# Making the delta-rule scan's operands beside the attention and loading them chunk by chunk

## The chip, the cores and the metric

The kernel runs on one core of a Trainium2 chip. It is written in Python against an explicit tile framework: the program allocates tiles in named pools, issues instructions to five engines (PE for matmuls, with a separate count PEld for its weight loads; DVE and ACT for element-wise work and reductions; POOL and SP, which here mostly issue DMA transfers), and a scheduler puts them into one fixed order per engine. The metric is the device time of one execution in microseconds; less is better.

## The reference, cut to what matters

One layer of a bidirectional trunk on 1024 tokens of width 1024, all in float32: a half-step feed-forward network, a mixing layer, a second half-step feed-forward network. The mixing layer projects its normed input once (`z = h @ w_in`). One part of the columns goes into attention (8 heads, three dilated bands), the other into RWKV-7, a delta-rule recurrence that runs forwards and backwards over the sequence, with its own decays and rates in each direction:

```python
u = u + mu_prev * (prev - u) + mu_next * (nxt - u)        # the "shift"
r, k, v, wd, ad, gd = jnp.split(u, cuts, axis=-1)         # receptance, key, value, low ranks
decay = jnp.exp(-jnp.exp(-jax.nn.softplus(-w_logit) - 0.5))
a = jax.nn.sigmoid(a0 + jnp.einsum('bsdr,drc->bsdc', ad, a2))
kk = kk / jnp.maximum(jnp.sqrt(jnp.sum(kk * kk, axis=-1, keepdims=True)), 1e-12)
k_dir = k[:, :, None, :] * (1.0 + (a - 1.0) * k_a)
...
def _rwkv7_step(state, inp):
    r, w, k, v, kk, kka = inp
    sa = jnp.einsum('dbhvk,dbhk->dbhv', state, kk)
    state = state * w[..., None, :] - sa[..., :, None] * kka[..., None, :] + v[..., :, None] * k[..., None, :]
    y = jnp.einsum('dbhvk,dbhk->dbhv', state, r)
```

`kk` is the normed key, `kka = kk * a` the rate, `k_dir` the key. The outputs of both directions are added, normed by group, given a bonus from `r`, `k_dir` and `v`, gated, and projected together with the attention's output.

## The kernel before, in words

**The scan in chunks.** The recurrence is not run token by token. The 1024 tokens are cut into 16 chunks of 64 (`C = 64`), two chunks to a block (`BLK = 2`, `TB = 128` tokens), 8 blocks, each in both directions. Channels lie on partitions: 512 channels are 4 tiles of 128, each a pair of heads of 64. With `cum` the running log decay inside a chunk, the chunk form needs four decayed operands: receptances `r * exp(cum)` and normed keys `kk * exp(cum one step earlier)` (the program's `pr`, side by side), rates and keys divided by the decay, `(1 + a) * kk * 0.5 * exp(-cum)` and `k_dir * exp(-cum)` (the program's `bk`), and the decay of the whole chunk, `gc`. From them come the matrix of products within a chunk (`lp`, masked to `lm`), whose inverse is built by doubling, and then the state goes from chunk to chunk.

**The order of the stages.** After the first feed-forward network and the low-rank projections, which store `cum` and the rates to DRAM (`lr_d`), comes the attention, 8 heads in a row (`attention`, with scores L713, bias and maximum L715, copies of the transposed weights L728, the last reduction `ss_a` of each head L763). After each head but the last `beside(h)` issues one stream of the RWKV projection (`project_rwkv` with `shift` and `stream`, L505 to L645), in the order `[4, 1, 5, 2, 6, 3, 7]`: column tiles 0 to 3 are receptances (0 comes earlier), 4 to 7 keys, 8 to 11 values. Then the scan begins: `prep` and `solve` of block 0, of block 1, the four value streams 8 to 11, and a loop over the blocks n with `merge`, `chain` and, ahead of need, `prep` and `solve` of block n + 3, with the projection of attended tokens among them (L1274 to L1333). The scheduler is free to weave these. The second feed-forward network follows.

**A key stream before.** ct 4 to 7 takes a shifted key tile of 128 channels x 1024 tokens (`us`). It loads the rates of both directions (`ra`, twice) and the receptances (`rr`) of the same channels. It makes the normed key `kr` (L611) and stores it. POOL adds the rates of the two directions (`rs`) and multiplies receptance by key (`rr`, L616); DVE multiplies the two (L618) for the bonus, which is stored. Then for each direction and each half of 512 tokens ACT makes `1 + (a - 1) * k_a` (L625) and DVE multiplies it by the key (`rb`, L626), stored by POOL; and for each direction DVE makes `(1 + a) * kr` over all 1024 tokens (`ra`, L628), stored by POOL.

**`prep` of a block before** (L818 to L876). For each direction SP loads `cum` (tile `th_w`), the rates `ka`, the keys `kd` (256 KB each) and receptances with normed keys (`in`, 512 KB). ACT makes `exp(cum)` (`e`, L840) and, in place, `exp(-cum)` (L841); DVE copies the chunks' last decay into `gc` (L843), and makes `pr` with two products (L845, L846; in the backward direction with a reversed view) and `bk` with two (L849, L851). A `bk` chunk has 192 columns: ACT copies the upper 64 partitions' rates behind the keys (L850), so that the odd head of a pair sees (keys, rates) where the even one sees (rates, keys). PE makes `lp` from `bk` and `pr` (L858), DVE masks (`lm`, L860), PE transposes `bk` (L866) and ACT copies that out (`bt`, L868). The PSUM pool of `prep` has three buffers. `solve` (L878 and on) runs its doubling on DVE (L894, L896); `merge` and `chain` hold the PE groups called st, y and xu; the state update on DVE is `sv` (L990).

**The value streams** (ct 8 to 11): shift (L537, L538), a reversed copy (L634), PE transposes (L640), ACT copies, and 8 stores each by SP.

The few lines of `prep` that the change takes out of the scan:

```python
A.activation(e4[:, :, :, 1:C + 1], chunks(cum), AF.Exp)
A.activation(flat(cum), flat(cum), AF.Exp, scale=-1.0)
ei = chunks(cum)
V.tensor_copy(gc[:, d], e4[:, :, :, C])
V.tensor_tensor(pt[:, :, :, 0:C], chunks(x["kk"]), e4[:, :, :, 0:C], op=OP.mult)
V.tensor_tensor(pt[:, :, :, C:], chunks(x["r"]), e4[:, :, :, 1:C + 1], op=OP.mult)
V.scalar_tensor_tensor(bb, chunks(ak[0]), 0.5, ei, op0=OP.mult, op1=OP.mult)
A.copy(bk[64:, :, :, 2 * C:], bk[64:, :, :, 0:C])
V.tensor_tensor(bk[:, :, :, C:2 * C], chunks(ak[1]), ei, op=OP.mult)
```

Of the kernel before, what the change touches and what calls it, by code (L numbers as in the profile page):

```python
# [10 lines left out]
F32 = mybir.dt.float32  # L11
F32R = mybir.dt.float32r
AF = mybir.ActivationFunctionType
# [150 lines left out]
class _Kernel:  # L164
# [340 lines left out]
    def project_rwkv(self, p, psum, x, blocks, wide=None):  # L505

        nc, V, A, T = self.nc, self.nc.vector, self.nc.scalar, self.nc.tensor
        for c0, n in blocks:
# [6 lines left out]
            if 4 <= c0 < 8:  # L515
                self.rates.append(wide.tile([128, S], F32, name="rs", tag="rr"))
            for ct in range(c0, c0 + n):
# [61 lines left out]
    def stream(self, p, psum, ct, y):  # L579
# [10 lines left out]
        elif ct < 8:  # L590
# [21 lines left out]
            self.nc.gpsimd.dma_start(self.rk_d[4 + i], kr)  # L612
            rates, r, both = self.rates[:2], *self.rates[2:]
            self.rates.clear()
            G.tensor_tensor(both, rates[0], rates[1][:, ::-1], op=OP.add)
            G.tensor_tensor(r, r, y, op=OP.mult)  # L616
# [3 lines left out]
            for d, a in enumerate(rates):  # L620
                turned = lambda z: z[:, ::-1] if d else z
                for half in range(2):
                    sl = slice(half * 512, half * 512 + 512)
                    b = p.tile([128, 512], F32, name="rb", tag="vts")
                    A.activation(b, a[:, sl], AF.Identity, scale=self.kah[:, i:i + 1], bias=self.ka1[:, i:i + 1])  # L625
                    V.tensor_tensor(b, b, turned(y)[:, sl], op=OP.mult)  # L626
                    self.nc.gpsimd.dma_start(self.ak_d[d][4 + i][:, sl], b)
                V.scalar_tensor_tensor(a, a, 1.0, turned(kr), op0=OP.add, op1=OP.mult)  # L628
                self.nc.gpsimd.dma_start(self.ak_d[d][i], a)
# [16 lines left out]


# [170 lines left out]
    def prep(self, n, p, psum, big):  # L818

        nc, V, A, T = self.nc, self.nc.vector, self.nc.scalar, self.nc.tensor  # L820
        flat = lambda z: z.rearrange("p a t -> p (a t)")
        chunks = lambda z: z.rearrange("p a (i t) -> p a i t", i=BLK)
        ls = slice(n * TB, (n + 1) * TB)
        lm = big.tile([128, 2, 2, BLK, 4, 128], F32, name="lm", tag="lm")
        gc = big.tile([128, 2, 4, BLK], F32, name="gc", tag="gc")
        blk = dict(lm=lm, pr=[], bt=[], gc=gc)
        for d in range(2):
            b = n if d == 0 else NC_ // BLK - 1 - n
            ts = slice(b * TB, (b + 1) * TB)
            cum = p.tile([128, 4, TB], F32, name="th_w", tag="th_w", bufs=2)  # L830
            self.load(cum, self.lr_d["w"][d][:, :, ls].rearrange("a p t -> p a t"))
            ak = [p.tile([128, 4, TB], F32, name=nm, tag=nm, bufs=b) for nm, b in (("ka", 2), ("kd", 1))]
            for j in range(2):
                self.load(ak[j], self.ak_d[d][4 * j:4 * j + 4, :, ls].rearrange("a p t -> p a t"))
# [640 lines left out]
```

## Time and profile before

Three runs took 2301.5, 2297.94 and 2296.86 us, median 2297.94. One execution was profiled; it gives no time of its own beside its span.

| | |
|---|---|
| median of the runs | 2297.94 us |
| span of the profiled execution | 2299.0 us |
| instructions in it | 41391 |
| PE busy (matmuls) | 2198.8 us, 96% |
| PE's weight loads | 1781.8 us, 77% |
| DVE busy | 1767.3 us, 77% |
| ACT busy | 1023.6 us, 45% |
| POOL busy | 537.0 us, 23% |

The stages lie in the span as follows: up to 915 us the first feed-forward network and the projections, 915 to 1183 the attention with the receptance and key streams, 1183 to 1292 the scan's start with the value streams, 1292 to 1480 its steady part, up to 1600 its last block and what follows it, and from 1700 the second feed-forward network.

In the lines of the profile a group is an engine, a line of the kernel, an operation, and the tile it writes with the tile it reads (out<-in); then partitions x elements, how many there were, busy time in us, mean ns of one. A wait is "engine, what it wanted to do and at which line <- the engine and line that it waited for". SP, POOL and the like with a "q" are queues of DMA transfers. Issuing a DMA is not counted in an engine's busy share, though a group of issues has a duration.

### The profile page before, as it was taken

The page shows a single profiled execution, that of the slowest core. Times are in us where ns is not written, and L with a number is a line of the kernel's source. Part 1 is how long each engine was busy: PE and PEld are TensorE (multiplying, and loading weights), DVE is VectorE, ACT ScalarE, POOL GpSimd, SP SyncE. Part 2 cuts the span into 40 slices and gives each one's busy share as a digit, 9 for nine tenths or more (in the row PEclk, how much of TensorE's full clock was granted, in tenths as well). Part 3 has the DMA queues.
Part 4 walks back from the last instruction along what each step waited for, and adds up shares of the span by engine and source line. Part 5 has one row for each costly group of instructions (what it writes and reads, how often), then busy time and mean ns, then how long its engine had stood idle before and what let it go on. Part 6 is the DMA issues. An engine that isn't in the chain of part 4 may idle for free. (4 is left out here: it accounts for less than half of the span.)

```text
span 2299.0 us, 41391 instructions
## 1 busy us (share of the span) xinstructions
PE 2198.8 (96%) x15556; PEld 1781.8 (77%) x15556; DVE 1767.3 (77%) x2893; ACT 1023.6 (45%) x1925; POOL 537.0 (23%) x673
## 2 busy tenths in 40 slices
PE   7999999999999998999998899999799999999998
PEld 5788888878877676777776777776678888888887
DVE  7999999865676254677679678747999999997566
ACT  5322323354567411666654644455442323335453
POOL 2354443410000011222221111122024444441000
PEclk9999999999999999999999799999899999999999
DMA  5354545486662513654467746357445454548665
GB/s 151 124 183 151 170 147 173 164 266 193 193 225 78 212 72 105 186 147 144 131 178 184 211 136 167 107 173 257 155 135 174 150 174 151 170 152 282 194 194 187
DMA packets 346700, 387.74 MB, mean 169 GB/s; under 512 B 73474, under 2 KB 249346, under 8 KB 346500
## 3 DMA queue, kind: packets, MB, share of 16 engines
q1 hardware_dynamic: 294928, 271.71, 39.2%
q0 software_dynamic: 31216, 100.73, 11.6%
q10 hardware_dynamic: 20356, 12.66, 1.8%
q8 instruction: 122, 2.00, 0.4%
q14 instruction: 78, 0.64, 0.1%
HBM read 258.06 MB, written 126.94 MB: 167 GB/s over the span
## 5 line engine op out<-in xcount | busy, mean ns | idle before, releaser
L81 PE MATMUL gu<-xh,wh 128*128 128x512 f32 x704 | 277.3, 394 | 4.6 <-ACT wh L186 4.5
L186 ACT ACTIVATE wh<-raw 128x512 fp32r<-128x512 f32 (+1 forms) x273 | 168.3, 627 | 252.3 <-PE gu L81 95.7
L81 PE MATMUL gu<-xl,wh 128*128 128x512 f32 x704 | 276.0, 392 | 0.0
L81 PE MATMUL gu<-xh,wl 128*128 128x512 f32 x704 | 275.9, 392 | 0.0
L187 DVE TENSOR_TENSOR wl<-raw,wh 128x512 fp32r<-128x512 f32 (+1 forms) x273 | 270.4, 994 | 3.7 <-ACT wh L186 3.0
L421 PE MATMUL pd<-gl,gwh 128*128 128x512 f32 x616 | 240.6, 391 | 2.6 <-DVE gl L187 2.6
L421 PE MATMUL pd<-gh,gwh 128*128 128x512 f32 x616 | 239.8, 390 | 0.6 <-DVE row L86 0.6
L421 PE MATMUL pd<-gh,gwl 128*128 128x512 f32 x616 | 240.1, 390 | 0.2 <-DVE gwl L187 0.2
L86 DVE TENSOR_TENSOR row<-gu,row 128x512 f32<-128x512 f32 x308 | 206.6, 683 | 25.8 <-PE gu L81 23.5
L187 DVE TENSOR_TENSOR gwl<-graw,gwh 128x512 fp32r<-128x512 f32 (+2 forms) x187 | 118.8, 643 | 124.0 <-ACT gwh L186 122.3
L116 POOL DMA_DIRECT2D d_hid<-row x154 | 84.7, 551 | 546.0 <-DVE row L114 524.2
L186 ACT ACTIVATE gwh<-graw 128x512 fp32r<-128x512 f32 (+2 forms) x187 | 103.1, 554 | 187.2 <-PE pd L421 151.3
L81 PEld LDWEIGHTS gu<-xh,wh 128*128 128x128 f32 x704 | 133.4, 190 | 33.6 <-ACT wh L186 5.6
L81 PEld LDWEIGHTS gu<-xh,wl 128*128 128x128 f32 x704 | 133.2, 189 | 27.7 <-DVE wl L187 0.2
L81 PEld LDWEIGHTS gu<-xl,wh 128*128 128x128 f32 x704 | 133.3, 189 | 27.4
L421 PEld LDWEIGHTS pd<-gl,gwh 128*128 128x128 f32 x616 | 115.7, 188 | 27.8 <-DVE gl L187 3.9
L421 PEld LDWEIGHTS pd<-gh,gwh 128*128 128x128 f32 x616 | 115.6, 188 | 25.5 <-DVE row L86 1.0
L421 PEld LDWEIGHTS pd<-gh,gwl 128*128 128x128 f32 x616 | 115.7, 188 | 24.1 <-DVE gwl L187 0.6
L187 DVE TENSOR_TENSOR gl<-raw,gh 128x512 fp32r<-128x512 f32 x160 | 114.7, 728 | 22.9 <-ACT gh L186 22.6
L94 ACT ACTIVATE row<-row 128x512 f32<-128x512 f32 x44 | 27.8, 633 | 212.0 <-DVE row L86 212.0
L145 POOL TENSOR_TENSOR ws<-ws 128x512 f32<-128x512 f32 x88 | 114.6, 1303 | 1.2
L186 ACT ACTIVATE gh<-raw 128x512 fp32r<-128x512 f32 x160 | 98.1, 622 | 35.5 <-DMA raw<-in_ffn_w_down_dram 22.8
(364 smaller groups left out, 5238.2 us busy)
## 6 DMA issues: line engine op xcount, KB each, us to landing
d_hid<-row POOLq DMA_DIRECT2D x154, 256.0 KB, 2.5
graw<-d_hid SPq DMA_DIRECT2D x132, 256.0 KB, 2.9
raw<-in_ffn_w_gate_dram SPq DMA_DIRECT2D x88, 256.0 KB, 3.1
raw<-in_ffn_w_up_dram SPq DMA_DIRECT2D x88, 256.0 KB, 3.6
ws<-in_ffn_w_down_dram SPq DMA_DIRECT2D x88, 256.0 KB, 4.1
d_ws<-ws POOLq DMA_DIRECT2D x88, 256.0 KB, 2.3
raw<-d_ws SPq DMA_DIRECT2D x88, 256.0 KB, 2.8
raw<-in_ffn_w_down_dram SPq DMA_DIRECT2D x66, 256.0 KB, 3.6
```

The costliest lines, as they stand in the source:

```text
L81: self.K.nc.tensor.matmul(ps, a[:, k, :], b[:, k, :], start=(k == 0 and i == 0), stop=(k == 3 and i == 2))
L86: add = lambda o, x: V.tensor_tensor(o, ps, x, op=OP.add)
L94: A.activation(y[:, 0], y[:, 0], AF.Silu)
L116: put = lambda n, y: G.dma_start(self.hid[n - 1, j // 2], y)
L145: G.tensor_tensor(o, a, b, op=OP.subtract)
L186: self.nc.scalar.activation(h, src, AF.Copy)
L187: (eng or self.nc.vector).tensor_tensor(l, src, h, op=OP.subtract)
L421: T.matmul(ps[x], a[:, ts], b, start=(m == 0 and k == 0), stop=(m == NM - 1 and k == 2))
```

## The change

The four decayed operands of all chunks are made in the key streams, beside the attention, and stored to DRAM in the layout in which the scan's matmuls read them; `prep` only loads them. In a key stream, a new function runs for each direction: in each half of 512 tokens ACT makes `1 + (a - 1) * k_a` and both exponentials, DVE makes the key, the rate (now in halves), two products for `pr` (tile `pk`, one buffer) and two for `bk` (tile `bk`, one buffer under the tag `u`), POOL copies the chunks' last decays into `gc`, which now lives through the scan in a pool of its own. POOL stores the `pk` tile in one transfer (512 KB), the lower 64 partitions of `bk` in one, and the upper 64 in two whose pieces are 64 floats long, which swap rates and keys on the way; thus `bk` in the scan is 128 wide for both heads of a pair. The key stream now loads `cum` too (two tiles `cu`); the normed keys, keys and rates are no longer stored by themselves. The sum of the rates and the product of receptance and key go from POOL to DVE.

```diff
+                for d in range(2):
+                    a = wide.tile([128, S], F32, name="cu", tag="cu")
+                    self.load(a, self.lr_d["w"][d][c0 - 4])
+                    self.rates.append(a)
...
-            self.nc.gpsimd.dma_start(self.rk_d[4 + i], kr)
...
-            G.tensor_tensor(both, rates[0], rates[1][:, ::-1], op=OP.add)
-            G.tensor_tensor(r, r, y, op=OP.mult)
+            V.tensor_tensor(both, rates[0], rates[1][:, ::-1], op=OP.add)
+            for d, a in enumerate(rates):
+                self.chunk_operands(p, i, d, a, cums[d], kr, y, r)
+            V.tensor_tensor(r, r, y, op=OP.mult)
...
-            for d, a in enumerate(rates):
-                turned = lambda z: z[:, ::-1] if d else z
-                for half in range(2):
-                    sl = slice(half * 512, half * 512 + 512)
-                    b = p.tile([128, 512], F32, name="rb", tag="vts")
-                    A.activation(b, a[:, sl], AF.Identity, scale=self.kah[:, i:i + 1], bias=self.ka1[:, i:i + 1])
-                    V.tensor_tensor(b, b, turned(y)[:, sl], op=OP.mult)
-                    self.nc.gpsimd.dma_start(self.ak_d[d][4 + i][:, sl], b)
-                V.scalar_tensor_tensor(a, a, 1.0, turned(kr), op0=OP.add, op1=OP.mult)
-                self.nc.gpsimd.dma_start(self.ak_d[d][i], a)
...
+    def chunk_operands(self, p, i, d, a, cum, kr, y, r):
...
+        for half in range(2):
+            sl = slice(half * 512, half * 512 + 512)
+            k = p.tile([128, 512], F32, name="rb", tag="vts")
+            A.activation(k, a[:, sl], AF.Identity, scale=self.kah[:, i:i + 1], bias=self.ka1[:, i:i + 1])
+            V.tensor_tensor(k, k, turned(y)[:, sl], op=OP.mult)
+            V.scalar_tensor_tensor(a[:, sl], a[:, sl], 1.0, turned(kr)[:, sl], op0=OP.add, op1=OP.mult)
+            e, c = self.e1, chunks(cum[:, sl])
+            A.activation(e[:, :, 1:C + 1], c, AF.Exp)
+            A.activation(cum[:, sl], cum[:, sl], AF.Exp, scale=-1.0)
+            nc.gpsimd.tensor_copy(self.gc[:, d, i, half * 8:half * 8 + 8], e[:, :, C])
+            pt = self.wide.tile([128, 8, 2, C], F32, name="pk", tag="pk", bufs=1)
+            V.tensor_tensor(pt[:, :, 0], chunks(turned(kr)[:, sl]), e[:, :, 0:C], op=OP.mult)
+            V.tensor_tensor(pt[:, :, 1], chunks(turned(r)[:, sl]), e[:, :, 1:C + 1], op=OP.mult)
+            nc.gpsimd.dma_start(self.pr_d[d][i][:, half * 1024:half * 1024 + 1024], pt.rearrange("p a b t -> p (a b t)"))
+            bk = p.tile([128, 8, 2, C], F32, name="bk", tag="u", bufs=1)
+            V.scalar_tensor_tensor(bk[:, :, 0], chunks(a[:, sl]), 0.5, c, op0=OP.mult, op1=OP.mult)
+            V.tensor_tensor(bk[:, :, 1], chunks(k), c, op=OP.mult)
+            out = self.bk_d[d][i][:, half * 1024:half * 1024 + 1024]
+            nc.gpsimd.dma_start(out[0:64], bk[0:64].rearrange("p a b t -> p (a b t)"))
+            up = out[64:128].rearrange("p (a b t) -> p a b t", b=2, t=C)
+            for q in range(2):
+                nc.gpsimd.dma_start(up[:, :, q], bk[64:128, :, 1 - q])
...
+            self.load(pt.rearrange("p a i t -> p a (i t)"), self.pr_d[d][:, :, ks].rearrange("a p t -> p a t"))
+            bk = p.tile([128, 4, BLK, 128], F32, name="bk", tag="bk", bufs=2)
+            self.load(bk.rearrange("p a i t -> p a (i t)"), self.bk_d[d][:, :, ks].rearrange("a p t -> p a t"))
```

The instructions' order on the engines follows from the scheduler. DVE before, in the attention beside the third key stream (rows are line, operation, out<-in and shape; `sb,nm` at L715 is an attention score's bias and maximum, `kr`, `rb`, `ra` are the stream's normed key, key and rate):

```order
L611 SCALAR_TENSOR_TENSOR kr<-us,c_rwkv_k_k,kt 128x512
L187 TENSOR_TENSOR zl<-zraw,zh 128x128 x3
L611 SCALAR_TENSOR_TENSOR kr<-us,c_rwkv_k_k,kt 128x512
L626 TENSOR_TENSOR rb<-rb,us 128x512
L628 SCALAR_TENSOR_TENSOR ra<-ra,kr 128x1024 x2
L715 ISA sb,nm<-s_10113,k_bias_7764 128x512
L715 ISA nm 128x1
```

DVE after, at the same place (L739 is what was L715, L616 what was L611, L653 and L654 the key and rate; `pk` and `bk` are the new products, `e` and `cu` the exponentials, `rr` the receptance):

```order
L654 SCALAR_TENSOR_TENSOR ra<-ra,kr 128x512
L616 SCALAR_TENSOR_TENSOR kr<-us,c_rwkv_k_k,kt 128x512
L660 TENSOR_TENSOR pk<-kr,e_7776 128x8x64
L664 SCALAR_TENSOR_TENSOR bk<-ra,cu 128x8x64
L665 TENSOR_TENSOR bk<-rb,cu 128x8x64
L654 SCALAR_TENSOR_TENSOR ra<-ra,kr 128x512
L739 ISA sb,nm<-s_10278,k_bias_7774 128x512
L739 ISA nm 128x1
L653 TENSOR_TENSOR rb<-rb,us 128x512
L654 SCALAR_TENSOR_TENSOR ra<-ra,kr 128x512
L660 TENSOR_TENSOR pk<-kr,e_7776 128x8x64
L661 TENSOR_TENSOR pk<-rr,e_7776 128x8x64
```

The products with the exponentials now stand between the attention's reductions. DVE before, at the attention's last reduction (`ss_a`) and the start of the scan (`us` is a value stream's shift, `vrev` its reversed copy, `gc` to `pr` are `prep` of block 0):

```order
L763 TENSOR_REDUCE ss_a<-far 128x8
L537 SCALAR_TENSOR_TENSOR us<-u,c_rwkv_mu_prev,us 128x1023
L1181 TENSOR_REDUCE unit<-ident 128x1
L538 SCALAR_TENSOR_TENSOR us<-u,c_rwkv_mu_next,us 128x1023
L187 TENSOR_TENSOR zl<-zraw,zh 128x128
L634 COPY vrev<-us 128x1024
L187 TENSOR_TENSOR zl<-zraw,zh 128x128
L843 COPY gc<-e_11074 128x8
L849 SCALAR_TENSOR_TENSOR bk<-ka,th_w 128x8x64
L851 TENSOR_TENSOR bk<-kd,th_w 128x8x64
L845 TENSOR_TENSOR pr<-in_11088,e_11074 128x8x64
L846 TENSOR_TENSOR pr<-in_11088,e_11074 128x8x64
```

DVE after, there (L787 is the last reduction, L542 and L543 the shift, L861 the masks of block 0 and 1, L895 the doubling of `solve`, L622 and L624 the sums that stood on POOL and the bonus):

```order
L661 TENSOR_TENSOR pk<-rr,e_7776 128x8x64
L622 TENSOR_TENSOR rr<-rr,us 128x1024
L624 TENSOR_TENSOR rs<-rs,rr 128x1024
L664 SCALAR_TENSOR_TENSOR bk<-ra,cu 128x8x64
L665 TENSOR_TENSOR bk<-rb,cu 128x8x64
L787 TENSOR_REDUCE ss_a<-far 128x8
L1180 TENSOR_REDUCE unit<-ident 128x1
L542 SCALAR_TENSOR_TENSOR us<-u,c_rwkv_mu_prev,us 128x1023
L543 SCALAR_TENSOR_TENSOR us<-u,c_rwkv_mu_next,us 128x1023
L630 COPY vrev<-us 128x1024
L861 TENSOR_TENSOR lm<-lp,k_tri 128x512 x13
L895 TENSOR_TENSOR ttmp<-X,Ti 128x31
```

The last products of a key stream stand ahead of the attention's last reduction, and behind it come masks at once, where the products of `prep` stood. The loads on SP's queue for block 0 before (in brackets what each waits for):

```order
L182 DMA th_w<-d_w_110 128x4x128 [waits PE_49]
L182 DMA ka<-d_ak_140 128x4x128 [waits DMASW7_49]
L182 DMA kd<-d_ak_140 128x4x128 [waits DMASW1_49,PE_49]
L182 DMA in_11088<-d_rk 128x8x128 [waits DMASW4_49,DMASW6_49,DMASW3_49,DMAHW3_49,PE_49,Pool_49]
L182 DMA th_w<-d_w_113 128x4x128 [waits DMAHW4_49]
```

And after:

```order
L182 DMA pr<-d_pr_140 128x4x256 [waits DMASW4_49,DMASW2_49,DMASW6_49,DMASW0_49,PE_49]
L182 DMA bk<-d_bk_146 128x4x256 [waits DMASW6_49,DMASW7_49,DMASW5_49,DVE_49]
L182 DMA pr<-d_pr_143 128x4x256 [waits DMASW4_49,DMASW2_49,DMAHW1_49,DMASW0_49,Pool_49]
L182 DMA bk<-d_bk_149 128x4x256 [waits DMASW7_49,DMASW6_49,DMAHW5_49,DMASW5_49,DMASW1_49]
L182 DMA pr<-d_pr_140 128x4x256 [waits DMAHW6_49,DVE_49]
```

Two loads of 512 KB for each direction stand in place of four, and they wait for the stores of the last key stream.

57 lines of the change are left out of this document (19 added, 38 removed).

## The prediction

> **What bounds the kernel now.** I read the stages first (busy time of each engine by window), then the waits inside the stages that the change touches, then the groups of instructions that it moves, and last the chain and the timeline where one stage hands over to the next. The columns below are the window, its length, the busy time of PE, PE's weight loads, DVE, ACT and POOL with instruction counts, the granted TensorE clock, the DMA share and GB/s.
>
> ```profile
> 915.00:1183.00 268.00, 261.07 (x2549) 208.23 (x2550) 193.02 (x470) 170.52 (x394) 69.36 (x75) 0.98 0.50 150
> 1183.00:1292.00 109.00, 92.14 (x1123) 77.14 (x1123) 80.19 (x215) 55.56 (x101) 15.28 (x30) 0.79 0.81 209
> 1292.00:1480.00 188.00, 177.17 (x3442) 147.06 (x3438) 148.30 (x439) 90.42 (x163) 26.06 (x51) 0.93 0.53 146
> ...
> 1600.00:1700.00 100.00, 84.70 (x394) 67.88 (x393) 90.61 (x141) 50.98 (x98) 3.89 (x6) 0.91 0.42 129
> ```
>
> The first row is the attention with the receptance and key streams beside it: PE is busy in 97% of it, DVE in 72%. The second is the scan's start-up, with the value streams: PE has 17 us idle and a mean clock of 0.79, DVE is busy in 74%. The third is the scan's steady part: PE 94%, DVE 79%. The last row lies behind the scan, where nothing is changed; it shows below how busy DVE can get. So the change takes DVE work out of two stages and puts it into a third, and PE leads in all three. How tightly DVE stands to PE is seen in the waits (engine, line waited for, us in total, times, longest): two of DVE and one of PE in the attention, then PE's in the start-up, then PE's in the steady part.
>
> ```profile
> DVE sb L715 <- PE s L714: 29.3, 25, 3.3
> DVE e L728 <- PE pt L727: 14.8, 19, 1.4
> ...
> PE s L713 <- DVE nm L715: 2.2, 3, 1.0
> ...
> PE vt L640 <- DVE us L538: 4.2, 2, 3.7
> PE lp L858 <- DVE lm L860: 4.2, 3, 3.2
> ...
> PE lp L858 <- DVE lm L860: 4.5, 5, 1.1
> ```
>
> In the attention DVE waits 44 us for PE, and PE hardly waits for DVE: DVE follows. In the scan PE waits for DVE 8.4 us in the start-up and 4.5 us in the steady part. A DVE instruction taken out of the scan is therefore worth much less than its duration.
>
> **The change part by part.** The groups that move, with busy time and mean ns; the first four and L843 are DVE work that leaves the scan, L840, L841 and L850 are ACT's; L618, L626 and L628 price what stays in the streams.
>
> ```profile
> L849 DVE SCALAR_TENSOR_TENSOR bk<-ka,th_w 128x512 f32<-128x512 f32 x16 | 11.0, 689 | 6.2 <-ACT th_w L841 6.1
> L845 DVE TENSOR_TENSOR pr<-in,e 128x512 f32<-128x512 f32 x16 | 11.0, 688 | 8.5 <-PE y L959 5.1 <-DMA in<-d_rk 3.4
> L851 DVE TENSOR_TENSOR bk<-kd,th_w 128x512 f32<-128x512 f32 x16 | 11.0, 685 | 0.0
> L846 DVE TENSOR_TENSOR pr<-in,e 128x512 f32<-128x512 f32 x16 | 10.9, 684 | 0.0
> L843 DVE COPY gc<-e 128x8 f32<-128x8 f32 x16 | 2.7, 169 | 2.2 <-ACT e L840 2.2
> ...
> L840 ACT ACTIVATE e<-th_w 128x512 f32<-128x512 f32 x16 | 10.1, 631 | 8.3 <-DMA th_w<-d_w 2.6 <-DVE ttmp L894 1.8 <-DVE Ti L896 1.8
> L850 ACT COPY bk<-bk 64x512 f32<-64x512 f32 x16 | 9.8, 614 | 3.3 <-DVE bk L849 3.1
> ...
> L626 DVE TENSOR_TENSOR rb<-rb,us 128x512 f32<-128x512 f32 x16 | 18.5, 1171 | 0.3 <-ACT rb L625 0.2
> L618 DVE TENSOR_TENSOR rs<-rs,rr 128x1024 f32<-128x1024 f32 x4 | 4.8, 1211 | 0.0
> L628 DVE SCALAR_TENSOR_TENSOR ra<-ra,kr 128x1024 f32<-128x1024 f32 x8 | 9.4, 1220 | 0.0
> ```
>
> *Attention.* Four key streams, two directions and two halves make 16 sets, as many as the scan had (8 blocks, two directions). Each brings four DVE instructions of 128x512: 64 x 0.687 = 44.0 us. The two sums of 128x1024 that go from POOL to DVE cost 8 x 1.211 = 9.7 us by L618, which has that shape. The rates' product is cut into halves: 16 x 0.689 - 8 x 1.220 = 1.3 us. But the POOL sums were not free for DVE, as the timeline of the last key stream shows (start, us, and in brackets the idle time ahead):
>
> ```profile
> 1156.51 2.38 POOL L616 TENSOR_TENSOR rr<-rr,us 128x1024 f32<-128x1024 f32 x1 [6.71 <-issue]
> ...
> 1156.56 3.48 DVE L626 TENSOR_TENSOR rb<-rb,us 128x512 f32<-128x512 f32 x2
> ```
>
> Two products of 0.685 us took 3.48 us while POOL read the same memory for 2.38 us. With the sum on DVE that stretch goes: L626 falls from 1.171 to about 0.685 us, 16 x 0.486 = -7.8 us. In sum DVE gets 44.0 + 9.7 + 1.3 - 7.8 = 47 us and stands at 240 of 268 us, 90%. Its idle 75 us shrink to 28, and what fills them is mostly waiting for PE, so much of the 47 us is covered. ACT gets 32 exponentials of 0.631 us, 20 us on 170.5, and stays at 71%: covered by its own idle time. What is queued behind the new DVE work are the score reductions L715; for them wait ACT's exponentials, and the next scores on PE, which have two PSUM banks. The price lies between these rows: DVE reached 91% in the window 1600:1700 above, which would give 240 / 0.906 = 265, no loss; in the busiest 40 us of the scan it reached 85%,
>
> ```profile
> 1320.00:1360.00 40.00, 38.36 (x778) 32.15 (x775) 34.07 (x104) 19.81 (x36) 5.62 (x11) 0.96 0.54 151
> ```
>
> which would give 240 / 0.85 = 283, +15 us. A gain is excluded, since PE keeps its work and its 97%. I take 88%, 273 us, **+5**: nearer the upper row, because DVE here mostly waited for PE.
>
> *The stores.* Loads of keys and rates in the scan go, stores of chunks come (queue, count, KB, us from issue to landing):
>
> ```profile
> in<-d_rk SPq DMA_DIRECT2D x16, 512.0 KB, 5.7
> ...
> d_ak<-ra POOLq DMA_DIRECT2D x8, 512.0 KB, 4.9
> ...
> ka<-d_ak SPq DMA_DIRECT2D x16, 256.0 KB, 5.1
> ...
> d_vt<-vts SPq DMA_DIRECT2D x32, 128.0 KB, 3.1
> ```
>
> POOL issues 64 stores instead of 28 (24 of keys and rates, 4 of normed keys); 32 of the new ones have pieces of 64 floats. No row on POOL has so many pieces. Its store of 128 pieces took 0.54 us and its load of 256 pieces 0.73:
>
> ```profile
> L1007 POOL DMA_DIRECT2D f_y<-d_y x16 | 11.6, 725 | 27.5 <-DMA wor<-in_w_out_dram 8.8 <-ACT yb L992 8.5 <-DVE xl L187 6.6
> ...
> L629 POOL DMA_DIRECT2D d_ak<-ra x8 | 4.3, 537 | 4.8 <-DVE ra L628 4.8
> ```
>
> By that slope 512 pieces are about 1.1 us (an estimate; ends 0.54 and 2.1). So POOL adds 32 x 0.54 + 32 x 1.1 - 28 x 0.54 = 37 us of issue and loses 8 sums of 2.38 us, 19 us: 69 + 18 = 87 of 268 us, nothing on the path, unless the attention's own POOL sums stand behind a store that waits for DVE.
>
> A rule speaks against these pieces. The Trainium skill, "DMA: Bandwidth & Descriptors", Specifications, gives 512 B as the least transfer for line rate. The trace agrees in kind: 128 KB in pieces of 256 B took 3.1 us (d_vt), 512 KB in longer rows 4.9 us. By it the 4 MB in such pieces go at a fraction of the rate; here they are spread over the attention, whose DMA share is 0.50, and I take nothing for it outside the rival below.
>
> *Start-up of the scan.* DVE loses the 26 products and 6 copies that stood between 1183 and 1292: 26 x 0.687 + 6 x 0.169 = 18.9 us. What the end of this stage hangs on is the last value stream and what follows it. The timeline (start, us, instruction, and in brackets the wait ahead of it):
>
> ```profile
> 1182.73 0.69 DVE L763 TENSOR_REDUCE ss_a<-far 128x8 f32<-128x512 f32 x1 [1.00 <-POOL e L1178]
> ...
> 1248.30 1.28 DVE L537 SCALAR_TENSOR_TENSOR us<-u,c_rwkv_mu_prev,us 128x1023 f32<-128x1023 f32 x1
> ...
> 1276.58 1.28 ACT L840 ACT_TABLE_LOAD   x1
> ...
> 1291.38 1.41 DVE L990 TENSOR_TENSOR sv<-st,gc 64x512 f32<-64x512 f32 x2 [0.69 <-PE st L959]
> ```
>
> Between the two stands a load in the chain of waits (start, us, what):
>
> ```profile
> 1260.68 6.63 DMA in<-d_rk
> 1267.34 0.69 DVE pr L845
> ```
>
> From the attention's last sum (1182.7) to the last stream's shift (1248.3) are 65.6 us. In the new order DVE has ahead of that shift: six shifts of 1.28 (7.7), three copies (2.1, at 0.69 each), sixteen masks and both whole solves,
>
> ```profile
> L860 DVE TENSOR_TENSOR lm<-lp,k_tri 128x512 f32<-128x512 f32 x24 | 15.8, 685 | 4.8 <-PE lp L858 4.7
> L894 DVE TENSOR_TENSOR ttmp<-X,Ti 128x126 f32<-128x126 f32 (+22 forms) x62 | 15.0, 251 | 1.0
> L896 DVE TENSOR_TENSOR Ti<-Ti,ttmp 128x126 f32<-128x126 f32 (+22 forms) x62 | 14.9, 252 | 1.1
> ```
>
> 16 x 0.685 = 11.0 and 29.9 us, and about 5 us of transposes and weight splits (an estimate from their count): 56 us. New in front of it is the way of the last set: store (4.9) and load (5.7), 10.6 us, of which DVE covers some 7.7 us (two sums of 1.21, three instructions of 0.69, two shifts, one copy). That makes 56 + 3 = 59 us, 7 earlier. The solves are complete by then, but the values still have to be stored and loaded, and the load ahead of 1267 remains, as a load of finished operands; behind it the product (0.69) and the table load (1.28) go. I take **-7**; the ends are -16 (all of the 18.9 us less the 3) and +3 (the last set's store and load wholly exposed, nothing gained).
>
> *Steady part.* DVE loses 38 products and 10 copies in 188 us, 38 x 0.687 + 10 x 0.169 = 27.8 us, ACT its two exponentials and a copy per set. On the chain stands one pair of them alone:
>
> ```profile
> 1340.67 0.69 DVE pr L845
> 1341.57 0.60 DVE pr L846
> ```
>
> Sure are thus 1.3 us; PE's 4.5 us for the masks bound the rest: **-5**. The ends are -11 (such a pair shortened in each of five blocks, 6.5, and the 4.5) and +2 (the loads, now straight into tiles that PE reads, come late once). The last block's chain and what follows it are unchanged.
>
> Sum: +5 - 7 - 5 = -7 us on the profiled span of 2299.0. The median of the runs is 2297.9, 1.1 us below that span; I take the difference as it is: **2291 us**, 0.3% faster. About 0.2% (4.6 us) is what a measurement of this kernel can tell from no change.
>
> **The rivals.**
>
> 1. *DVE becomes the bound of the attention; slower.* For it: 90% DVE beside 97% PE, all in fixed order, and the last head: the sums before it and in it lie at 1149.8 and 1182.7, 32.9 us apart, and a quarter of the 47 us (11.8) falls there on a DVE that has an eighth of the stage's 193.0 us, 24.1, in each head: 36 us do not fit into 32.9. Price: 283 - 268 = +15 and +3 for that head, less 9 given back in the scan: +9, 2307 us. It decides when DVE's share of the attention stays at 85% or below while that stage grows. Against it: PE's 2.2 us of waiting for reductions. Chance 0.27.
>
> 2. *No change.* PE and the values' way through memory keep the scan's pace; the start-up gives 3, the steady part 2, the attention takes 5: 2298 us. For it: the small waits of PE for DVE above. Chance 0.23.
>
> 3. *The small pieces hold DVE up; slower.* The tile for rates and keys has one buffer. Its three stores take about 0.54 + 2 x 1.1 us to issue and 3.1 to land, 5.8 us, and between two such tiles DVE has two or three products and a split, 2 to 3 us, where no attention work stands between: up to 3 us at one place in each set pair, 8 pairs, half of it covered, +12. With the scan's -12 and the +5: 2303 us. The skill's rule named above would give this way. Against it: DMA share 0.50. Chance 0.06.
>
> **How the numbers follow.** The forecast has 0.44, with its own range of 2277 to 2293. Faster by over 0.2%: 0.44; within: 0.23; slower: 0.27 + 0.06 = 0.33. The lowest sum of the ends is 0 - 16 - 11 = -27 (2271), the highest +18 + 3 + 2 = +23 (2321); leaving out a tenth at each side gives 2276 to 2312.
>
> **What would show it.** In the new profile the attention's last sum should come 3 to 8 us later, with DVE at 88 to 90% and PE's waits for reductions under 10 us; the rates' products at 0.69 us each. From there to the first state update (sv) should take about 101 us instead of 108.7, and the steady part some 183 instead of 188. Wrong would be: the attention more than 12 us longer (rival 1), no shortening between last sum and first state update (rival 2), or DVE waiting for stores before its bk products (rival 3).

## The result and the profile after

The change made the kernel slower: 2356.1 us (median of 4 runs) against 2297.4 for the kernel before, a ratio of 1.0251 with a 95% interval of 1.0222 to 1.0281. The forecast was 2291 us, its range ended at 2312. The profiled execution spans 2351.0 us, 52 more than that of before.

Four marks in the timeline cut the difference into stages: the attention's last sum `ss_a`, the first and the last state update `sv`, and the first subtraction of the second feed-forward network's weights (DVE, L61). Starts in us, one profiled execution each, some experiments included. Stage times of one execution vary: in e16 and e17, two experiments below that leave the scan as it was, it took 238.9 and 243.1 us from the first to the last `sv` against 248.3 before, in e16 at a granted clock of 0.98 instead of 0.93. Differences of a few us between rows are therefore not resolved; the medians decide.

| kernel | last ss_a | first sv | last sv | L61 |
|---|---|---|---|---|
| before | 1182.7 | 1291.4 | 1539.7 | 1657.9 |
| after | 1228.7 | 1331.3 | 1577.2 | 1709.3 |
| e1_pad | 1223.4 | 1327.7 | 1577.2 | 1694.4 |
| e4_in_pad | 1224.2 | 1319.2 | 1570.0 | 1684.9 |
| e5_dummy | 1209.4 | 1320.0 | 1570.2 | 1691.1 |
| e17_half | 1193.3 | 1301.2 | 1544.3 | 1672.4 |
| e12_reverse | 1177.0 | 1286.0 | 1552.7 | 1680.3 |
| e18_bare2 | 1182.4 | 1283.0 | 1534.5 | 1651.2 |

After against before: the attention ends 46.0 us later; from there to the first state update 102.6 us instead of 108.7; from the first to the last 245.8 instead of 248.3; and from the last to L61 132.1 instead of 118.2. The scan gave 8.6 us, the attention took 46, and 13.9 were lost behind the scan, where the prediction expected no change. The stages of the kernel after by window (columns as before: window, length, PE, weight loads, DVE, ACT, POOL, clock, DMA share, GB/s):

```profile
915.00:1229.00 314.00, 275.19 (x2544) 216.97 (x2542) 228.90 (x553) 189.36 (x421) 78.25 (x118) 0.92 0.56 163
1229.00:1331.00 102.00, 85.68 (x1104) 71.36 (x1106) 65.15 (x196) 44.35 (x80) 14.29 (x30) 0.85 0.66 183
1331.00:1578.00 247.00, 228.17 (x4631) 191.44 (x4628) 149.31 (x450) 97.34 (x179) 39.09 (x71) 0.93 0.46 140
1578.00:1709.00 131.00, 111.62 (x638) 84.05 (x636) 96.19 (x150) 67.63 (x139) 21.32 (x23) 0.93 0.61 205
```

DVE got 35.9 us more in the attention (228.9 against 193.0), less than the 47 forecast. But its idle time there did not shrink from 75 to 28 us; it is 85 us. PE, which was idle for 7 us of 268, is idle for 39 of 314. What it waits for, and what DVE waits for, in the waits of the attention (engine, line <- engine, line, us, times, longest):

```profile
DVE sb L739 <- PE s L738: 26.7, 24, 3.4
DVE e L752 <- PE pt L751: 15.1, 12, 1.5
...
PE s L737 <- DVE sb L683: 11.8, 3, 4.5
PE s L737 <- DVE nm L739: 4.8, 8, 1.1
```

The three waits of PE for `sb` at L683 (the far scores' subtraction) are all of one kind: before each, DVE runs the same four products and a sum. The timeline of the first shows it (start, us, instruction, in brackets the idle time ahead):

```profile
993.67 0.69 DVE L664 SCALAR_TENSOR_TENSOR bk<-ra,cu 128x512 f32<-128x512 f32 x1 [0.52 <-DMA d_bk<-bk]
...
995.48 0.68 DVE L661 TENSOR_TENSOR pk<-rr,e 128x512 f32<-128x512 f32 x1
...
996.24 1.22 DVE L622 TENSOR_TENSOR rr<-rr,us 128x1024 f32<-128x1024 f32 x1
...
997.45 0.68 DVE L683 TENSOR_TENSOR sb<-s,n 128x512 f32<-128x512 f32 x1
...
998.28 0.76 PE L737 MATMUL s<-kh,sq 128*128 128x512 f32 x1 [4.51 <-DVE sb L683]
```

From 993.67 on DVE is hardly idle, but four operand products (two of them shown) and a sum of 1.22 us stand in its fixed order ahead of the one subtraction for which PE waits. Elsewhere in the stage DVE still waits for PE's scores and transposes.

At the end of the attention the loss has another cause. ACT and PE stand still for 16 and 19 us:

```profile
1224.18 0.69 DVE L664 SCALAR_TENSOR_TENSOR bk<-ra,cu 128x512 f32<-128x512 f32 x1 [2.29 <-DMA d_bk<-bk]
...
1226.86 0.73 POOL L670 DMA_DIRECT2D d_bk<-bk  x1
...
1230.91 0.60 ACT L540 ACTIVATE u<-zr 128x512 f32<-128x512 f32 x1 [16.18 <-POOL Ti L891]
...
1232.13 0.79 PE L528 MATMUL zr<-xh,zh 128*128 128x512 f32 x1 [19.25 <-ACT us L541]
```

ACT wants to copy the first value stream's projection into the tile `u` (L540), PE to go on with the next projection into the PSUM bank that this copy frees. `u` has one buffer under the tag `u`, and `bk` of the change is put into the same buffer. So `u` is free only when the fourth `bk` tile of the last key stream has been stored: the last store is issued at 1226.86, a store of this kind takes 4.2 us to land, and at 1230.91 ACT goes on. The profile names POOL's `Ti` because its semaphore came last; experiment 2 shows that it is the buffer.

The loss behind the scan is seen in POOL's timeline. Before, the loads of finished outputs (`f_y`) start among the last chunks' loads:

```profile
1500.73 1.19 POOL L930 DMA_DIRECT2D uv<-d_vt  x2 [1.48 <-ACT yb L992]
1501.91 0.74 POOL L1007 DMA_DIRECT2D f_y<-d_y  x1
1511.46 2.89 POOL L1007 DMA_DIRECT2D f_y<-d_y  x4 [8.82 <-DMA wor<-in_w_out_dram]
```

There the first comes 38 us ahead of the last state update (1539.7). After, they stand behind the last chunk's loads, and the first comes 5 us ahead of it (1577.2):

```profile
1571.08 1.19 POOL L931 DMA_DIRECT2D uv<-d_vt  x2 [1.48 <-ACT yb L993]
1572.26 3.55 POOL L1008 DMA_DIRECT2D f_y<-d_y  x5
```

### The profile page after: what moved, and what is told of

It reads as the page before. It is cut to its first block, busy times and chain, and to the rows that moved or that the text cites. A ratio compares the mean times of both kernels' runs of the same rounds, so it can differ in the third digit from the quotient of the medians.

```text
span 2351.0 us, 41395 instructions
## 1 busy us (share of the span) xinstructions
PE 2209.6 (94%) x15556; PEld 1787.3 (76%) x15556; DVE 1760.2 (75%) x2893; ACT 1013.3 (43%) x1907; POOL 546.1 (23%) x717
## 5 line engine op out<-in xcount | busy, mean ns | idle before, releaser
L187 DVE TENSOR_TENSOR wl<-raw,wh 128x512 fp32r<-128x512 f32 (+1 forms) x273 | 271.7, 998 | 4.4 <-ACT wh L186 3.5
L187 DVE TENSOR_TENSOR gwl<-graw,gwh 128x512 fp32r<-128x512 f32 (+2 forms) x187 | 118.8, 642 | 127.3 <-ACT gwh L186 123.9
L421 PEld LDWEIGHTS pd<-gl,gwh 128*128 128x128 f32 x616 | 115.6, 188 | 27.9 <-DVE gl L187 4.3
L187 DVE TENSOR_TENSOR gl<-raw,gh 128x512 fp32r<-128x512 f32 x160 | 112.3, 713 | 20.6 <-ACT gh L186 20.2
```

The lines of the kernel that those rows point to most:

```text
L187: (eng or self.nc.vector).tensor_tensor(l, src, h, op=OP.subtract)
L421: T.matmul(ps[x], a[:, ts], b, start=(m == 0 and k == 0), stop=(m == NM - 1 and k == 2))
```

## The experiments

**Two buffers.** The theory after the result had three separate costs: DVE's products ahead of the attention's reductions, the buffer of `u`, and the place of the `f_y` tiles, which lie in memory that the scan frees; the scan's loads need 20 KB per partition less of it, so that everything above moved. Its rivals: all of it is DVE's added work and the rest follows; or the stores in small pieces.

*e1_pad.*

```diff
         self.unit = p.tile([128, 2, 16], F32, name="unit")
+        p.tile([128, 5016], F32, name="pad")
```

> The changed kernel with an unused tile of 20 KB per partition in the pool of the scan's loads, so that the tiles of the last stage lie again where they lay before the change. Theory (three separate costs: products ahead of the attention's reductions, some +27 us; the shift's tile u that must wait for the stores of bk at the attention's end, some +15; the outputs' tiles f_y that came to lie on the last block's operands, +14): the first f_y loads are issued ahead of the last chunk's loads again, 2356 - 14 = 2342 us. Rival (all of it is DVE's added work, the late finish only follows from it): 2356, no change.

Measured: 2341.2 us, ratio to before 1.0196 (1.0164 to 1.0227), 15 us less than the change. An unused tile, which adds no instruction, does this. From the last `sv` to L61 it takes 117.3 us again. POOL's timeline:

```profile
1539.64 0.72 POOL L1008 DMA_DIRECT2D f_y<-d_y  x1
1550.10 2.84 POOL L1008 DMA_DIRECT2D f_y<-d_y  x4 [9.73 <-issue]
...
1570.54 1.19 POOL L931 DMA_DIRECT2D uv<-d_vt  x2 [1.48 <-ACT yb L993]
```

*e2_inplace.*

```diff
-            bk = p.tile([128, 8, 2, C], F32, name="bk", tag="u", bufs=1)
-            V.scalar_tensor_tensor(bk[:, :, 0], chunks(a[:, sl]), 0.5, c, op0=OP.mult, op1=OP.mult)
-            V.tensor_tensor(bk[:, :, 1], chunks(k), c, op=OP.mult)
+            V.scalar_tensor_tensor(a[:, sl], a[:, sl], 0.5, cum[:, sl], op0=OP.mult, op1=OP.mult)
+            V.tensor_tensor(k, k, cum[:, sl], op=OP.mult)
...
+            for q, z in enumerate((chunks(a[:, sl]), chunks(k))):
+                nc.gpsimd.dma_start(out[0:64, :, q], z[0:64])
+                nc.gpsimd.dma_start(out[64:128, :, 1 - q], z[64:128])
```

> The changed kernel with the two products for bk made in place, in the tiles of rates and keys, and stored from there in four stores of 64 partitions (64 stores with pieces of 256 bytes instead of 32), so that no bk tile shares the buffer of u. Theory of three costs: ACT's wait of 16 us ahead of the first value stream goes, PE's 19 us with it, 2356 - 15 = 2341 us. Rival DVE's work: unchanged, 2356. Rival small pieces: twice as many of them, 2360 or more.

Measured: 2341.8 us, 1.0183 (1.0150 to 1.0215), 14 us less, with twice as many small stores. PE's longest waits between 1180 and 1235 us are now 4.5 and 2.1 us:

```profile
PE vt L636 <- ACT vts L638: 5.2, 2, 4.5
PE zr L528 <- ACT us L541: 2.1, 1, 2.1
```

*e3_pool_sums.* The two sums back on POOL (`V.` to `G.` in two lines).

> The changed kernel with the sum of the rates and the product of receptance and key back on POOL. Theory of three costs: DVE loses 9.7 us in the attention, part of it comes back as slower DVE products while POOL reads, and the 4.5 us waits of PE for the far score's sum get shorter by 1 to 2 us each: 2350 us. Rival DVE's work as the bound: the whole 9.7 us, 2346. Rival small pieces: 2356.

Measured: 2356.8 us, 1.0262 (1.0223 to 1.0301): no difference. This does not say that DVE's work is free, since DVE got no less of it: in the attention it is busy for 232.7 us here and for 228.9 in the changed kernel. Some of its instructions are longer in this run; the longest at L714 took 2.65 us, where it is 1.22 in the changed kernel.

*e4_in_pad.* Both edits, of the first and the second experiment.

> The changed kernel with both edits, products in place and the unused tile. Theory of three costs: they add up, 2356 - 15 - 14 = 2327 us. Rival DVE's work: 2356. Rival small pieces: over 2356.

Measured: 2332.0 us, 1.0141 (1.0114 to 1.0168). By the ratios 25 us of the 58 are gone, about the sum of the two, and 32 remain. In its profiled execution the attention is 41 us longer than before and the scan's start 14 us shorter (95.1 us); part of that is work that PE now does before the attention's last sum.

**DVE's price in the attention.**

*e5_dummy.* On the kernel before:

```diff
+                    pt = self.wide.tile([128, 2, 512], F32, name="pk", tag="pk", bufs=1)
+                    for q in range(4):
+                        V.tensor_tensor(pt[:, q % 2], turned(kr)[:, sl], y[:, sl], op=OP.mult)
```

> The kernel before with 64 more products of 128x512 on DVE in the key streams (four for each direction and half, key times normed key into a tile that nobody reads), 44 us of DVE work as in the change, but with no store, no exponential and no load more; the scan is left as it was. Theory that DVE's work in the attention costs time nearly in full, since DVE's waits for PE there are round trips and no slack: 30 to 44 us more, 2297.6 + 35 = 2333 us. Rival (the prediction's own step: DVE's idle time covers it, and stores, exponentials or loads make the change slow): 2297.6 + 5 = 2303.

Measured: 1.0112 (1.0077 to 1.0147), 26 us more (2326.4). *e17_half* is the same with `range(2)`.

> The fifth experiment with half its idle products on DVE (32 of 128x512 in the key streams of the kernel before, 22 us). If DVE's waits in the attention take up work until a threshold: within 4 us of the kernel before, 2300 us or less. If each product costs the same share, 0.6 of its duration as in the fifth: 2298 + 13 = 2311 us.

Measured: 2310.6 us, 1.0058 (1.0037 to 1.0079), 13 us more. Half the work costs half: no threshold is seen, and each us of added products costs 0.6. The attention's windows of both, half and whole:

```profile
915.00:1193.00 278.00, 268.73 (x2582) 213.15 (x2583) 214.01 (x507) 172.02 (x399) 68.02 (x74) 0.97 0.50 149
...
915.00:1209.00 294.00, 275.53 (x2598) 219.91 (x2599) 232.29 (x535) 171.41 (x395) 66.67 (x77) 0.96 0.47 140
```

DVE's idle time went from 75 us (before) to 64 and 62 while its work grew by 21 and 39: most of the work was added to the stage, not put into its gaps. The two waits for PE that the prediction had read as room, 44 us in all, are still there in e5, with 39.5 us:

```profile
DVE sb L719 <- PE s L718: 26.3, 24, 3.7
DVE e L732 <- PE pt L731: 13.2, 16, 1.9
```

*e7_nobk.* The fourth experiment without its two in-place products by `cum`.

> The fourth experiment (products in place, unused tile) without the 32 products that decay rates and keys, everything else kept, their stores and exponentials too; it leaves out this decay. DVE loses 22 us in the attention. Theory of full cost: 2332 - 20 = 2312 us. Rival (stores, exponentials and loads): 2330.

Measured: 2315.9 us, 1.0062 (1.0038 to 1.0086), about 18 less than e4 by the ratios, for 22 us of DVE.

*e8_spread.* `rest()` holds the second direction's operands and the bonus and is called in the next head.

> The fourth experiment with the backward direction's operands and the bonus put off to the next head's stream, so that heads with a key stream and heads with a receptance stream get DVE work more evenly. If the unevenness is what costs (key heads with DVE at 83%, the others at 55 to 65%): 2332 - 8 = 2324 us. If the sum of DVE's work counts: 2332.

Measured: 2334.8 us, 1.0148 (1.0113 to 1.0183): no difference. Spreading the work more evenly gave nothing. In the profiled execution the attention's last sum came 15 us earlier than in e4 (1209.0), and the way to the first state update took 17 us longer (112.5), so that the end of the attention changed too; how evenly the heads have the work is not tested alone.

**What the scan can give back.**

*e6_bare.* On the kernel before:

```diff
+            self.load(pt.rearrange("p a i t -> p (a i t)").rearrange("p (a t) -> p a t", t=TB), self.rk_d[:, :, ts].rearrange("a p t -> p a t"))
+            bk = p.tile([128, 4, BLK, 128], F32, name="bk", tag="bk", bufs=2)
+            self.load(bk.rearrange("p a i t -> p (a i t)").rearrange("p (a t) -> p a t", t=TB), self.ak_d[d][:, :, ls].rearrange("a p t -> p a t"))
...
-            V.tensor_tensor(pt[:, :, :, 0:C], chunks(x["kk"]), e4[:, :, :, 0:C], op=OP.mult)
-            V.tensor_tensor(pt[:, :, :, C:], chunks(x["r"]), e4[:, :, :, 1:C + 1], op=OP.mult)
```

> The kernel before with the scan part of the change alone: the scan loads 512 KB twice for each block and direction straight into pr and bk and makes no exponentials, products or copies; the streams stay as they were, with plain factors of 0.001 in place of 1 in two of their products. It leaves out the decays, and the columns of pr and bk hold undecayed operands in another order. It bounds what the scan can give back. Theory: the start gives 10 to 14 us, the steady part nothing since PE leads it, 2297.6 - 12 = 2286 us, with 248 us between first and last state update as before. Rival (the prediction): start 7 to 16 us and steady part 5, 243 us between the updates, 2283 or less.

Measured: 2303.8 us, 1.0023 (1.0001 to 1.0045): no gain. *e18_bare2* has the tile `gc` where it was (`big.tile`, and a `memset`).

> The sixth experiment (scan part alone, decays left out) with the chunk decays' tile where it was in the kernel before, and POOL writing a constant into it, so that the outputs' tiles lie as before and the first f_y loads are issued ahead of the last chunk's loads again. If the 8 us that the sixth had gained by the first state update were given back by the late f_y loads: 2304 - 7 = 2296 to 2289 us, some 5 us faster than before. If the finish does not depend on it: 2303.

Measured: 2299.0 us, 1.0000 (0.9979 to 1.0021). The scan's windows, and below them that of the steady part in the kernel before:

```profile
1182.00:1283.00 101.00, 84.97 (x1110) 70.40 (x1110) 63.84 (x190) 42.67 (x80) 16.01 (x35) 0.87 0.77 198
1283.00:1535.00 252.00, 229.53 (x4643) 190.46 (x4640) 156.24 (x466) 103.65 (x192) 44.57 (x81) 0.95 0.51 148
```

```profile
1291.00:1540.00 249.00, 232.41 (x4641) 193.34 (x4637) 174.08 (x516) 119.65 (x217) 43.75 (x75) 0.93 0.54 154
```

The first state update comes 8.4 us earlier than before (1283.0), but from there to the last it takes 251.5 us instead of 248.3, with DVE busy for 156 us instead of 174. Less DVE work does not shorten this stage. In the measured times nothing is left, within 5 us.

*e11_rev_rates* and *e12_reverse* go the other way, on the kernel before. The second:

```diff
-                    V.tensor_tensor(b, b, turned(y)[:, sl], op=OP.mult)
...
-                V.scalar_tensor_tensor(a, a, 1.0, turned(kr), op0=OP.add, op1=OP.mult)
...
+            V.scalar_tensor_tensor(ak[0], ak[0], 1.0, x["kk"], op0=OP.add, op1=OP.mult)
...
+            V.tensor_tensor(ak[1], ak[1], x["k"], op=OP.mult)
```

> The opposite of the change for one product: the kernel before with the rates' product, (1 + a) times normed key, taken out of the key streams (8 x 1.22 us of DVE and 8 stores less beside the attention) and made in the scan's preparation (16 x 0.69 us of DVE, rates loaded from where they lie). Theory (a DVE us beside the attention costs 0.65 us, in the scan's steady part nothing, at its start a part): 2298 - 6 + 2 = 2294 us. Rival (the prediction's price of 0.1 in the attention): 2298 + 2 = 2300.

> The opposite of the change for two products: rates and keys are both made in the scan's preparation (32 x 0.69 us of DVE more there, one load wider, one buffer less for the rates), 28 us of DVE work leave the key streams. Theory: 2298 - 18 + 5 = 2285 us, faster than both kernels. Rival (the prediction's price): 2298 + 4 = 2302.

Measured: 2313.8 us, 1.0078 (1.0059 to 1.0096), and 2322.5 us, 1.0115 (1.0095 to 1.0135): both slower, against the theory. In the second the attention ends 5.8 us earlier, and from there to L61 it takes 503 us instead of 475. The products taken out had lasted 28 us, but DVE is busy for only 14 us less (178.8 against 193.0), because other instructions of DVE got longer (the splits at L187: 552 ns instead of 374). Windows of the attention and of the steady part:

```profile
915.00:1177.00 262.00, 256.40 (x2537) 205.00 (x2538) 178.83 (x443) 169.16 (x391) 63.63 (x71) 0.97 0.48 145
...
1286.00:1553.00 267.00, 236.14 (x4870) 197.53 (x4868) 185.61 (x539) 122.12 (x221) 45.05 (x78) 0.92 0.55 156
```

The steady part of e12 has 12 us more of DVE (185.6 against 174.1) and takes 18 us longer, but it also lacks a buffer for the rates. In e11, which has that buffer, the stage takes 248.6 us; there DVE got no more work in it (175.3 us), and the loss lies before and behind it (116.0 us from `ss_a` to the first `sv`, 126.2 from the last `sv` to L61). What a us of DVE costs in the steady part is thus not shown. In the attention a us of DVE less, by the busy time, gave 0.4 us in e12 and 0.5 in e11 (3.9 us for 8.1).

**Transfers and exponentials**, added to the kernel before.

*e9_act*: `A.activation(pt[:, q], kr[:, sl], AF.Exp)` twice for each direction and half.

> The kernel before with 32 more exponentials of 128x512 on ACT in the key streams (two for each direction and half, of the normed key, into a tile that nobody reads), 20 us of ACT work as in the change; DVE and the scan as before. Theory that DVE's order is what costs: ACT's idle time covers them, 2298 + 4 = 2302 us at most. Rival (ACT, which sits in the same chain of score, exponential and transpose, costs as much as DVE): 2298 + 13 = 2311.

Measured: 2295.4 us, 0.9995 (0.9982 to 1.0008). ACT's 20 us cost nothing that can be measured.

*e10_dma*, *e15_dma_rows* (its small pieces as rows of 2 KB) and *e16_dma_loads* (its loads alone):

```diff
+                    cu = wide.tile([128, S], F32, name="cu", tag="cu")
+                    self.load(cu, self.lr_d["w"][d][c0 - 4])
...
+                    nc.gpsimd.dma_start(self.pr_d[d][i][:, hs], kr)
+                    nc.gpsimd.dma_start(self.bk_d[d][i][0:64, hs], kr[0:64])
...
+                    for q in range(2):
+                        nc.gpsimd.dma_start(up[:, :, q], kc[:, :, 1 - q])
```

> The kernel before with the transfers of the change added to its own: two more loads of 512 KB in each key stream, and for each direction and half one store of 512 KB, one of 256 KB and two of 128 KB in pieces of 256 bytes, all from the normed key; no engine computes more. Theory: 2298 + 3 = 2301 us at most. Rival (queues and small pieces carry the rest of the loss): 2298 + 12 = 2310.

> The tenth experiment (only transfers added; 2348 us) with its 32 stores of 256-byte pieces in rows of 2 KB instead, the same bytes. If the small pieces cause the 52 us: 2310 us or less. If it is the bytes, the queues or the normed key's buffer, held by the stores: 2340 or more.

> The tenth experiment with its eight added loads alone, no added store. If the stores cause the 52 us: 2300 us, within 4 of the kernel before. If the loads ahead of the weights on SP's queue do: 2320 or more.

Measured: 2348.5 us, 1.0226 (1.0202 to 1.0250); 2335.7, 1.0169 (1.0136 to 1.0203); and 2299.0, 1.0014 (0.9990 to 1.0037). The loads cost nothing that can be measured. The stores, which here come on top of those of before (16 MB more, where the change writes 6 more), cost 39 us with long rows and some 13 more with small pieces. They all come from the tile of the normed key, but no wait of DVE for its buffer stands in the trace. How the stores may reach the path is seen in the run with long rows: its DMA answer and its waits of ACT up to 1180 us,

```profile
zraw<-in_w_in_dram SPq DMA_DIRECT2D x84, 64.0 KB, 4.0
```

```profile
ACT zh L186 <- DMA zraw<-in_w_in_dram: 27.9, 17, 6.6
```

and the same two lines in the kernel before:

```profile
zraw<-in_w_in_dram SPq DMA_DIRECT2D x78, 64.0 KB, 2.1
```

```profile
ACT zh L186 <- DMA zraw<-in_w_in_dram: 4.4, 2, 3.2
```

The projection's weights, 64 KB each, land after 4.0 us, where they took 2.1 in the kernel before, and ACT, which also makes the attention's exponentials, waits for them for 27.9 us instead of 4.4. The changed kernel shows little of this: its weights land after 2.3 us, and ACT waits 8.5 us for them.

*e13_noprod*: the fourth experiment without any product with exponentials, `pk`'s store taken from `kr`. *e14_rows*: the fourth experiment with stores in rows of 2 KB.

> The fourth experiment (products in place, unused tile; 2332 us) without any of the 64 products with exponentials: rates and keys are stored undecayed, and the store of receptances and normed keys takes its 512 KB straight from the normed key; it leaves out the decays. Loads, exponentials and stores stay as many and as large. If DVE's products carry the loss: 2332 - 28 = 2304 us or less. If the transfers carry it: 2320 or more.

> The fourth experiment with its 64 stores of rates and keys in rows of 2 KB in place of pieces of 256 bytes, as many stores and bytes, the same work on DVE (factors of 0.0005 and 0.001 keep the numbers small); it leaves out the order of the columns that the scan needs. If the small pieces cost much: 2332 - 12 = 2320 us. If the products do: 2332, within 4.

Measured: 2316.5 us, 1.0079 (1.0056 to 1.0101), and 2330.2 us, 1.0147 (1.0111 to 1.0184). Without the 44 us of products 14 us go, no more than without the 22 of e7, and the time lies between the two that had been expected; ACT's wait for `zraw` is then 16.8 us (3.7 in e4). A reading of this, not shown, is that stores and products stand behind one another: where one is taken out, the other is met. Row length makes no difference to the time, within 10 us.

## Why the prediction was wrong

**"So much of the 47 us is covered": failed, and the largest error.** The prediction read DVE's 44 us of waiting for PE as room and let DVE settle at 88% of a stage of 273 us, +5. In the run DVE is busy for 73% of a stage of 314. Experiments 5 and 17 show that the waits are no room: idle products cost 0.6 us per us, where the prediction took 5 / 47, 0.1, and the waits remain. In e4 DVE is busy as long as in e5 (232 us in both, 193 before), and in e5 that cost 26 us; the prediction's +5 and even its upper end of +18 were too small. A reading that fits the timeline at 993 us is that these waits are the other half of a round trip (scores, reduction, exponential, transpose, copy) in which each engine waits for the other in a fixed order. That PE hardly waits for an engine then says that the engine is just fast enough, not that it has time.

**The products beside POOL's sums: right in number only.** The products at L653 take 0.684 us each with the sums on DVE; 0.685 were forecast. But in experiment 3, with the sums back on POOL, they take 0.684 us too, and other instructions of DVE are longer. That the sums' place made L653 shorter is not shown; what stands beside them changed as well.

**"Nothing on the path" for the stores: failed.** The prediction named the condition under which they would be (a queue or a buffer), and in its third rival the one buffer of `bk`, but priced only DVE's wait for it (4.1 us in all after). It did not look up which tile shares that buffer: `u`, for which ACT and then PE wait 16 and 19 us. Experiment 2 gives its price, 14 us. The issue of a store in small pieces, estimated at 1.1 us, took 0.73.

The third rival's mechanism, small pieces, is not seen in this kernel. In the changed kernel a store of 128 KB in pieces of 256 bytes landed after 4.2 us:

```profile
d_bk<-bk POOLq DMA_DIRECT2D x16, 256.0 KB, 4.5
d_bk<-bk POOLq DMA_DIRECT2D x32, 128.0 KB, 4.2
```

and in e14 the same 128 KB in rows of 2 KB after 4.1 and 4.6 us, with the same time as e4, which has the pieces (ratios 1.0147 and 1.0141; the rival's price was 12 us). The rule of the Trainium skill, "DMA: Bandwidth & Descriptors", Specifications (512 B at least for line rate), shows in the time only where the transfers are denser: between e10 and e15, 13 us, at a DMA share of 0.66 in the attention against 0.56 in the changed kernel.

**"What follows it is unchanged": failed.** 13.9 us were lost there, and an unused tile brings back 15. The prediction followed the order of instructions up to the scan's end, and not that a smaller pool moves all tiles that are put on top of it. Experiment 1 shows it.

**Start-up -7: the size was right** (-6.1 after, -8.4 in e18). **Steady part -5: not resolved**, -2.5 after and +3.2 in e18, where the unchanged scans of e16 and e5 took 238.9 and 250.2. As a whole the scan part is worth nothing that can be measured (e18), so that the change had no gain to pay with.

**Rival 1** had the right stage and direction, and its sign came true: DVE's share stayed below 85% while the stage grew. Its mechanism did not: DVE is idle for 85 us and does not bound the stage by its work. It was priced at +15 for the stage and +3 for the last head, where the stage got 46 us longer.

**The range.** A tenth of its 50 us left out at each side gives 2276 to 2316, not to 2312; the result lies beyond either.

**Open** is how the 32 us of e4 divide between products and stores. Products alone cost 26 (e5), taking them out gives 14 to 18 (e7, e13), and exponentials and loads cost nothing that can be measured (e9, e16). For the 18 us that e13 still loses there remain the stores and the 7 us of other work that DVE keeps there (199.6 us against 193.0); but the stores were only measured alone in larger number (e10, e15), and not taken out of the changed kernel.

## What to carry to other kernels

Idle time of an engine that waits for the leading engine need not be room: before moving work there, put idle instructions of that size into the stage and measure (here 0.6 us per us, for half and whole alike). For each new tile look up which other tiles share its buffer, and who waits when its last store is late; and after a change in a pool's size look at the stages whose tiles lie on that memory later. Price the gain by itself too: a version that only leaves the work out (e18) would have shown first that there was nothing to win.

## What the runs showed of the hardware

After a pause PE runs at half its clock for some us. In the changed kernel (windows before, in and behind the pause of 19 us):

```profile
1195.00:1213.00 18.00, 17.88 (x165) 13.58 (x163) 14.67 (x41) 12.39 (x32) 5.22 (x10) 1.00 0.37 113
1213.00:1232.00 19.00, 0.00 (x0) 0.00 (x0) 10.56 (x17) 2.35 (x5) 11.41 (x22) 0.58 0.87 270
1232.00:1236.00 4.00, 3.87 (x11) 2.73 (x13) 2.75 (x3) 1.15 (x3) 0.00 (x0) 0.50 1.03 351
```

The granted clock is 1.00 ahead of the pause and 0.50 in the 4 us behind it (0.94 in the 4 us after those), and products of 128x512 follow one another by 0.43 us, where they do by 0.23 us at 1202 us:

```profile
1232.72 0.63 PE L528 MATMUL zr<-xl,zh 128*128 128x512 f32 x1
1233.15 0.63 PE L528 MATMUL zr<-xh,zl 128*128 128x512 f32 x1
```

This agrees with the Trainium skill, "TensorE: Matmul & The Clock Gate", Part 1, which states half the clock after an idle window. Thus a wait of PE can cost more than its length: PE's busy time in the attention grew from 261 to 275 us for about as many instructions; up to the pause at 1213 us the mean granted clock is 0.94, where it was 0.98 before.
